# A decoder layer on one core: splits placed around the first softplus, first weights cast on VectorE in smaller first loads, and the products of the first step reordered

## The chip, the cores and the metric

The kernel runs on one core of one Trainium2 chip. The metric is the device time of one execution in microseconds, the median of several runs. Lower is better.

## The reference

The reference computes one layer of a hybrid decoder for 512 tokens and a model width of 1024, in fp32. One combined projection of the residual stream `x` gives the queries, keys and values of three causal mixers (differential attention, stick-breaking attention, dilated window attention) and three gate vectors. The branches are projected, gated and summed, go through an output projection and a LayerNorm, and then a squared-ReLU MLP and a gated input embedding follow, with a second LayerNorm. The change touches the start: the first columns of the projection, and the first head of stick-breaking attention.

```
proj = x @ w_in                                   # first columns used here: sb_q, sb_k, sb_v
z = einsum('bhqd,bhkd->bhqk', q, k) * d ** -0.5   # 8 heads, d = 64
log_keep = where(before, log_sigmoid(-z), 0)      # minus a softplus
later = reverse_cumsum(log_keep) - log_keep
a = where(before, exp(log_sigmoid(z) + later), 0)
out = a @ v
```

## The kernel before

**Splits.** Every fp32 matrix that TensorE multiplies is split in two fp32r halves: a high part (a copy that rounds) and a low part (the matrix minus its high part). A product is then three matmuls: high by high, high by low, low by high. For weights, `split_next` makes the high part `wh` on ScalarE (ACT, line 227) and the low part `wl` on VectorE (DVE, line 228), for a chunk of 128x1024 at a time. The raw chunks come by DMA on SyncE's queue (SP) into a ring of four buffers (`RAW`), and the halves go to a ring of seven (`RING`). `pump(limit, most)` writes out up to `most` splits, and `fill` the loads that fit.

**Items.** The program is a list of items. An item is one group of matmuls into a PSUM bank (`mm`) and the evacuation of that bank (`ev`), which is written out at the start of the next item. Most items use the two banks `mm`, so an item can begin only when the evacuation of the item before the last has read its bank. A chunk of weights is named here after what it feeds:

- item 0: `first_item`, the first two column tiles (queries and keys of head pair 0, "Q0" and "K0"). It takes its eight chunks of `x` and five loads of weights in turn (lines 296 to 324), 24 pairs of matmuls;
- item 1: Q1, and item 2: K1 (queries and keys of head pair 1), one chunk each, 24 matmuls each (lines 87 to 89);
- items 3 to 6: the stick-breaking values `sb_v` for four blocks of tokens, from four chunks V1 to V4 that all four items share (lines 337 to 339);
- items 7 to 10: Q2, K2, Q3, K3, one chunk each.

**Attention between the items.** `step()` runs generators of attention work, once at the start of each item from item 2 on and once in the middle of an item's matmuls. Head 0 of stick-breaking (`sb_head`) starts in the middle of item 1: it multiplies queries by keys into three banks and then computes a softplus for bank 2, and later (a half item or more each) for banks 1 and 0. A softplus is three passes on ACT (absolute value at line 1015, exponential at 1016, logarithm at 1017) and then a chain on DVE: line 1018 (sum `e`), 1021 (`sph`, the high part), 1022 (`spl`, the low part), and sums for the banks before it (lines 1031 to 1041). TensorE then multiplies these by triangular matrices (lines 1048 and 1052).

**Order.** A planner orders the instructions of each engine when the kernel is built: of those it believes ready, the one written first in the program goes first. Tiles of the common pool of 42 slots are handed out in the order of the program, so an evacuation that is written behind a softplus is also queued behind it. `tc.issue_after(i)` adds that what follows is queued behind `i` where it is on the same engine. The list `tie` holds the last ACT and the last DVE instruction of head 0's first softplus (bank 2), and `issue_split` queues each split behind these two; `tie` is emptied in item 4. The splits of V2 to V4, Q2, K2 and Q3 are written after that softplus, so they stand behind it, and they are free to stand between the softplus of bank 2 and those of banks 1 and 0.

**Start.** Nine bf16 matmuls on zeros (line 845) run while the first loads come. The loads from the fifth on wait for the fifth of these. Item 0 takes `x` chunk k, and with chunks 0, 1, 3, 5 and 7 a load of weights (256 columns with 0 and 7, 512 columns, for two k, with the others).

Of the kernel before, what the change touches and what calls it, by code (L numbers as in the profile page):

```python
# [55 lines left out]
def trunk(tc, a, out):  # L56
    nc = tc.nc
    es = ExitStack()
    with es:
# [23 lines left out]
        def at_bank():  # L83
            return psum.tile([P, 512], F32, name=nm("at"), tag="at", bufs=6)
# [62 lines left out]
        def load(src, w, own=False):  # L147
            s = {"src": src, "w": w, "uses": 0, "own": own}
            loads.append(s)
            return s  # L150
# [9 lines left out]
        def chunk_of(s):  # L160
            c = {"from": s, "w": s["w"]}
            s["uses"] += 1
            chunks.append(c)
            return c
# [50 lines left out]
        def split_next():  # L215
            c = chunks[st["split"]]
            w = c["w"]
            if c.get("dst") is None:
                h = ring.tile([P, 1024], F32R, name=nm("wh"), tag="wh", bufs=RING)
                lo = ring.tile([P, 1024], F32R, name=nm("wl"), tag="wl", bufs=RING)  # L220
                parts = [(h[:, :w], lo[:, :w], 0, w)]
                c["h"], c["l"] = parts[0][:2]
            else:
                parts = c["dst"]
            for h, lo, a0, a1 in parts:
                raw = c["from"]["raw"][:, a0:a1]
                nc.scalar.copy(h, raw)  # L227
                i = nc.vector.tensor_sub(lo, raw, h.bitcast(F32))  # L228
                st["low"] = getattr(i, "ins", i)
            c["from"]["uses"] -= 1  # L230
            st["split"] += 1
# [12 lines left out]
        def item(cs, mm, ev, need=None, bank=None):  # L244
            items.append({"c": cs, "mm": mm, "ev": ev, "need": need, "bank": bank})
# [55 lines left out]
        def first_item():  # L301

            w = a["w0"].rearrange("p k m -> p (k m)")
            cs = {}
            for k in range(8):
                x_chunk(k)
                if k in (0, 1, 3, 5, 7):
                    n = 256 if k in (0, 7) else 512
                    c = chunk_of(load(w[:, 256 * k:256 * k + n], n, True))
                    for i in range(n // 256):  # L310
                        cs[k + i] = (c, 256 * i)

            def mm(ps):
                for k in range(8):
                    c, o = cs[k]
                    for i, (m, x) in enumerate((("h", xh), ("l", xh), ("h", xl))):
                        for t in range(2):
                            nc.tensor.matmul(ps[t], c[m][:, o + t * P:o + t * P + P], x[k], start=k == 0 and i == 0,
                                             stop=k == 7 and i == 2, skip_group_check=True)

            def ev(ps):
                for t in range(2):
                    t_evac(*order[t][1:])(ps[t])
            item([cs[k][0] for k in (0, 1, 3, 5, 7)], mm, ev, bank=lambda: (at_bank(), at_bank()))

        def v_items(nv, name, g):
            cs = [chunk(a["wv"][nv, c].rearrange("p k n -> p (k n)"), 1024) for c in range(4)]
# [664 lines left out]
        def sb_head(hd):  # L992
            pr, side = hd // 2, hd % 2
            rs = (A, B)[side]
            while ("sb_q", pr) not in T or ("sb_k", pr) not in T:
                yield
            blk = [(0, 0, 0, 512), (1, 1, 0, 384), (2, 2, 0, 256), (3, 2, 256, 256)]
            bank = [at_bank() for _ in range(3)]
            for kb, bi, c0, n in reversed(blk):
                ps = bank[bi][:, c0:c0 + n]  # L1000
                mm_pair(ps, T["sb_k", pr], T["sb_q", pr], side, slice(kb * P, kb * P + P), slice(S - n, S),
                        kb != 2, False)
                if kb == 3:
                    nc.tensor.matmul(ps, identb, mask_b.rearrange("p a b -> p (a b)"), start=False, stop=False,
                                     skip_group_check=True)
                else:
                    nc.tensor.matmul(ps[:, 0:P], identb, mask_b[:, 1, :], start=False, stop=False,
                                     skip_group_check=True)
            w = [512, 384, 512]
            sph, spl, later = {}, {}, {}  # L1010
            for bi in (2, 1, 0):
                n = w[bi]
                ps = bank[bi][:, :n]
                e = slot("e")[:, :n]
                nc.scalar.activation(e, ps, AF.Abs)
                nc.scalar.activation(e, e, AF.Exp, scale=-1.0)
                ln = nc.scalar.activation(e, e, AF.Ln, bias=1.0)
                nc.vector.scalar_tensor_tensor(e, ps, 0.0, e, op0=OP.max, op1=OP.add)
                h = slot("sph", F32R)[:, :n]
                lo = slot("spl", F32R)[:, :n]  # L1020
                nc.vector.tensor_copy(h, e)
                low = nc.vector.tensor_sub(lo, e, h.bitcast(F32))
                if hd == 0 and bi == 2:

                    tie[:] = [getattr(i, "ins", i) for i in (ln, low)]
                sph[bi], spl[bi] = h, lo

                if bi == 2:
                    later[2] = (256, (h[:, HC], lo[:, HC]))
                    sm = slot("sm")[:, HB]  # L1030
                    nc.vector.tensor_add(sm, e[:, HB], e[:, HC])
                    hl = slot("smp", F32R)
                    nc.vector.tensor_copy(hl[:, HB], sm)
                    nc.vector.tensor_sub(hl[:, HC], sm, hl[:, HB].bitcast(F32))
                    later[1] = (256, (hl[:, HB], hl[:, HC]))
                elif bi == 1:
                    nc.vector.tensor_add(e[:, 128:384], e[:, 128:384], sm)
                    h = slot("smh", F32R)[:, :n]
                    lo = slot("sml", F32R)[:, :n]
                    nc.vector.tensor_copy(h, e)  # L1040
                    nc.vector.tensor_sub(lo, e, h.bitcast(F32))
                    later[0] = (384, (h, lo))
                yield
            ah, al = {}, {}
            for kb, bi, c0, n in reversed(blk):
                ps = bank[bi][:, c0:c0 + n]
                for hl in (sph, spl):
                    nc.tensor.matmul(ps, tri_r, hl[bi][:, c0:c0 + n], start=False, stop=False, skip_group_check=True)
                if kb < 3:
                    n2, hl = later[kb]  # L1050
                    for t in hl:
                        nc.tensor.matmul(bank[bi][:, c0 + n - n2:c0 + n], ones_r, t, start=False, stop=False,
                                         skip_group_check=True)
                if kb == 3:
                    continue
                n = w[bi]
                e = slot("a")[:, :n]
                nc.scalar.activation(e, bank[bi][:, :n], AF.Exp)
                h = slot("ah", F32R)[:, :n]
                lo = slot("al", F32R)[:, :n]  # L1060
                nc.vector.tensor_copy(h, e)
                nc.vector.tensor_sub(lo, e, h.bitcast(F32))
                ah[bi], al[bi] = h, lo
                if kb != 1:
                    yield
            while ("sb_v", 0, 3) not in V:
                yield
            po = at_bank()
            for kb, bi, c0, n in blk:
                v = V["sb_v", 0, kb][hd // 4][:, hd % 4]  # L1070
                nc.tensor.matmul(po[:, S - n:S], v.rearrange("p two d -> p (two d)"), ah[bi][:, c0:c0 + n],
                                 start=kb == 0, stop=False, skip_group_check=True)
                nc.tensor.matmul(po[A, S - n:S], v[:, 0, :], al[bi][:, c0:c0 + n], start=False, stop=kb == 3,
                                 skip_group_check=True)
            done = 4 + pr in oT
            if not done:
                oT[4 + pr] = slot("oT")
            t = slot("ot")
            nc.scalar.copy(t[A], po[B, :])
            nc.vector.tensor_add(oT[4 + pr][rs, :], po[A, :], t[A])  # L1080
            if done:
                split_sb(pr)
            yield
# [242 lines left out]
        for n, it in enumerate(items):  # L1326
# [9 lines left out]
            if prev is not None:  # L1336
                prev[0]["ev"](prev[1])

            pump(freed, 1 if n < 10 and n != 2 else 2)
            if n == 4:  # L1340
                tie.clear()
                with tc.issue_after(st["load"]):
                    load_consts()
            if n == 10:
# [128 lines left out]
```

## Time and profile before

| what | value |
|---|---|
| median of 3 runs | 1089.22 us (1088.9 to 1090.16) |
| the profiled execution | 1088.82 us |
| its span in the profile | 1087.1 us |
| TensorE busy | 1074.0 us, 99% of the span |
| VectorE, ScalarE busy | 691.8 us, 477.6 us |
| DMA | 105.71 MB, mean 97 GB/s |
| granted TensorE clock, mean | 0.996 |

The profiled execution lasted 1.72 us longer than its span and lies 0.40 us under the median. PE is TensorE's matmuls, PEld its weight loads. A line of the timeline gives the start, the duration, the engine, the line of the kernel, the operation, the tiles written and read, the shapes, and in brackets how long the engine was idle before it and what ended that idle time.

### The profile page before, as it was taken

Reading aid. Unit: us, or ns where it says so; the run is one execution under the profiler, and the core shown is the slowest. Engines: PE = TensorE matmul, PEld = TensorE weight load, DVE = VectorE, ACT = ScalarE, POOL = GpSimd, SP = SyncE. Lnnn points to the kernel's source line nnn. Section 1 sums busy time; section 2 is a strip of 40 time slices with the busy share of each in tenths; the row PEclk is TensorE's granted clock in tenths of the full one; section 3 lists DMA queues with packets and bytes.
Section 4 is the critical chain, followed back from the end, with each engine's and each line's share of the span. In section 5 each row is a group of like instructions: output and inputs, shape, how many; then the busy total and the mean of one; then the engine's idle time right before and its main releaser. Section 6 shows DMA issues by size and latency. Waiting matters only on the chain.

```text
span 1087.1 us, 13105 instructions
## 1 busy us (share of the span) xinstructions
PE 1074.0 (99%) x4991; PEld 894.2 (82%) x4991; DVE 691.8 (64%) x1245; ACT 477.6 (44%) x795; POOL 31.3 (3%) x55
## 2 busy tenths in 40 slices
PE   9899999999999999999999999999999999999997
PEld 6788788999888888888888888888888888888886
DVE  5788577657453757655444463866686686686676
ACT  6665445335232545454333232323554454454441
POOL 0000200000000000000000020110000000000000
PEclk9999999999999999999999999999999999999998
DMA  7432412031322113222233352253222422322402
GB/s 251 128 108 75 117 59 94 24 116 63 112 78 78 60 38 107 68 78 87 90 99 103 98 203 97 82 180 103 82 97 80 134 97 79 135 96 79 135 1 78
DMA packets 32431, 105.71 MB, mean 97 GB/s; under 512 B 4378, under 2 KB 5290, under 8 KB 32368
## 3 DMA queue, kind: packets, MB, share of 16 engines
q1 hardware_dynamic: 29424, 96.91, 27.4%
q0 software_dynamic: 2368, 7.05, 2.0%
q8 instruction: 39, 0.64, 0.2%
q10 hardware_dynamic: 576, 0.92, 0.2%
q14 instruction: 24, 0.20, 0.1%
HBM read 102.74 MB, written 2.12 MB: 96 GB/s over the span
## 4 chain that ended last, share of the span: by engine, by line
PE 94%; DVE 3%; DMA 1%; ACT 1%; issue 1%; DVEq 0%; SPq 0%
PE mm L87 17%; PE mm L89 17%; PE mm L88 17%; PE mm L337 3%; PE mm L339 3%; PE mm L338 3%; PE mm L679 2%; PE mm L681 2%; PE mm L680 2%; PE at L679 2%; PE at L681 2%; PE at L680 2%; PE mm L510 1%; PE mm L574 1%; PE mm L575 1%; PE mm L509 1%
## 5 line engine op out<-in xcount | busy, mean ns | idle before, releaser
L227 ACT CAST wh<-raw 128x1024 fp32r<-128x1024 f32 (+1 forms) x173 | 178.2, 1032 | 290.1 <-PE mm L88 222.8
L228 DVE TENSOR_TENSOR wl<-raw,wh 128x1024 fp32r<-128x1024 f32 (+1 forms) x173 | 206.1, 1196 | 104.6 <-ACT wh L227 100.6
L87 PE MATMUL mm<-xhT,wh 128*128 128x512 f32 x496 | 196.5, 396 | 0.0
L89 PE MATMUL mm<-xhT,wl 128*128 128x512 f32 x496 | 194.2, 391 | 0.1
L88 PE MATMUL mm<-xlT,wh 128*128 128x512 f32 x496 | 193.8, 391 | 0.0
L89 PEld LDWEIGHTS mm<-xhT,wl 128*128 128x128 f32 x496 | 93.1, 188 | 20.2 <-DVE wl L228 0.5
L87 PEld LDWEIGHTS mm<-xhT,wh 128*128 128x128 f32 x496 | 93.3, 188 | 19.5 <-issue 1.1
L88 PEld LDWEIGHTS mm<-xlT,wh 128*128 128x128 f32 x496 | 93.3, 188 | 17.8
L88 PE MATMUL mm<-x1lT,wh 128*128 128x512 f32 x256 | 99.6, 389 | 0.0
L89 PE MATMUL mm<-x1hT,wl 128*128 128x512 f32 x256 | 99.6, 389 | 0.0
L87 PE MATMUL mm<-x1hT,wh 128*128 128x512 f32 x256 | 99.6, 389 | 0.0
L337 PE MATMUL mm<-wh,xhT 128*128 128x512 f32 x160 | 65.5, 409 | 2.4 <-DVE sb_kb L108 2.3
L339 PE MATMUL mm<-wh,xlT 128*128 128x512 f32 x160 | 63.6, 398 | 0.0
L338 PE MATMUL mm<-wl,xhT 128*128 128x512 f32 x160 | 63.6, 397 | 0.0
L89 PEld LDWEIGHTS mm<-x1hT,wl 128*128 128x128 f32 x256 | 48.1, 188 | 10.1
L88 PEld LDWEIGHTS mm<-x1lT,wh 128*128 128x128 f32 x256 | 48.1, 188 | 10.0
L87 PEld LDWEIGHTS mm<-x1hT,wh 128*128 128x128 f32 x256 | 48.0, 188 | 9.9
L227 ACT CAST wh<-wsum 128x1024 fp32r<-128x1024 f32 x28 | 29.5, 1055 | 52.5 <-PE mm L88 49.3
L228 DVE TENSOR_TENSOR wl<-wsum,wh 128x1024 fp32r<-128x1024 f32 x28 | 34.2, 1222 | 24.2 <-ACT wh L227 23.6
L337 PEld LDWEIGHTS mm<-wh,xhT 128*128 128x128 f32 x160 | 38.2, 239 | 6.4 <-issue 2.7
L339 PEld LDWEIGHTS mm<-wh,xlT 128*128 128x128 f32 x160 | 38.3, 239 | 4.0
L338 PEld LDWEIGHTS mm<-wl,xhT 128*128 128x128 f32 x160 | 38.5, 241 | 3.5
(348 smaller groups left out, 1969.1 us busy)
## 6 DMA issues: line engine op xcount, KB each, us to landing
raw<-in_wt_dram SPq DMA_DIRECT2D x62, 512.0 KB, 3.4
raw<-in_wu_dram SPq DMA_DIRECT2D x32, 512.0 KB, 3.4
raw<-in_wd_dram SPq DMA_DIRECT2D x32, 512.0 KB, 3.3
raw<-in_wv_dram SPq DMA_DIRECT2D x20, 512.0 KB, 3.4
raw<-in_wb_dram SPq DMA_DIRECT2D x8, 512.0 KB, 3.3
raw<-in_wo_dram SPq DMA_DIRECT2D x8, 512.0 KB, 4.0
raw<-in_wg_dram SPq DMA_DIRECT2D x8, 512.0 KB, 3.9
rawx<-in_xT_dram SPq DMA_DIRECT2D x8, 256.0 KB, 5.1
```

Of the source, the lines that this page charges most:

```text
L87: nc.tensor.matmul(ps, wh, xh, start=start, stop=False, skip_group_check=True)
L88: nc.tensor.matmul(ps, wh, xl, start=False, stop=False, skip_group_check=True)
L89: nc.tensor.matmul(ps, wl, xh, start=False, stop=stop, skip_group_check=True)
L227: nc.scalar.copy(h, raw)
L228: i = nc.vector.tensor_sub(lo, raw, h.bitcast(F32))
L337: nc.tensor.matmul(ps, x1, c["h"][:, s], start=k == 0, stop=False)
L338: nc.tensor.matmul(ps, x1, c["l"][:, s], start=False, stop=False)
L339: nc.tensor.matmul(ps, x2, c["h"][:, s], start=False, stop=k == 7)
L509: nc.tensor.matmul(ps, h[:, q], c["l"][:, s], start=False, stop=False)
L679: nc.tensor.matmul(ps, h[:, q], c["h"][:, s], start=go, stop=False, skip_group_check=True)
L680: nc.tensor.matmul(ps, h[:, q], c["l"][:, s], start=False, stop=False, skip_group_check=True)
L681: nc.tensor.matmul(ps, lo[:, q], c["h"][:, s], start=False, stop=end, skip_group_check=True)
```

## The change

Three edits at the start of the kernel. First, the splits around head 0's softplus: item 1 writes out three of them instead of one (V1, V2, V3, ahead of the softplus of bank 2), item 2 one instead of two (V4), items 3 and 4 none, and items 5 to 8 one each (Q2, K2, Q3, K3). The first absolute value is queued behind the last cast written before it. `tie` is renewed by each of the three softplus of head 0 and emptied in item 8 instead of item 4, so that the splits of Q2, K2, Q3 and K3 are queued behind the softplus of bank 0. Second, in item 0 the first cast of weights moves from ACT to DVE, and the five loads of weights are 256, 256, 512, 512, 512 columns (with `x` chunks 0, 1, 2, 4, 6) instead of 256, 512, 512, 512, 256. Third, in item 0 the product of high weights by low `x` comes ahead of that of low weights by high `x`.

```diff
@@ split_next
-                nc.scalar.copy(h, raw)
+                i = nc.vector.tensor_copy(h, raw) if c.get("dve") else nc.scalar.copy(h, raw)
+                st["cast"] = getattr(i, "ins", i)
@@ first_item
-                if k in (0, 1, 3, 5, 7):
-                    n = 256 if k in (0, 7) else 512
+                if k in (0, 1, 2, 4, 6):
+                    n = 256 if k < 2 else 512
                     c = chunk_of(load(w[:, 256 * k:256 * k + n], n, True))
+                    c["dve"] = k == 0
...
-                    for i, (m, x) in enumerate((("h", xh), ("l", xh), ("h", xl))):
+                    for i, (m, x) in enumerate((("h", xh), ("h", xl), ("l", xh))):
...
-            item([cs[k][0] for k in (0, 1, 3, 5, 7)], mm, ev, bank=lambda: (at_bank(), at_bank()))
+            item([cs[k][0] for k in (0, 1, 2, 4, 6)], mm, ev, bank=lambda: (at_bank(), at_bank()))
@@ sb_head
-                nc.scalar.activation(e, ps, AF.Abs)
+                with ExitStack() as behind:
+                    if hd == 0 and bi == 2:
+
+                        behind.enter_context(tc.issue_after(st["cast"]))
+                    nc.scalar.activation(e, ps, AF.Abs)
...
-                if hd == 0 and bi == 2:
+                if hd == 0:
 
                     tie[:] = [getattr(i, "ins", i) for i in (ln, low)]
@@ the loop over items
-            pump(freed, 1 if n < 10 and n != 2 else 2)
+            pump(freed, {1: 3, 3: 0, 4: 0}.get(n, 1 if n < 10 else 2))
+            if n == 8:
+                tie.clear()
             if n == 4:
-                tie.clear()
                 with tc.issue_after(st["load"]):
                     load_consts()
```

## The prediction

> **What bounds the kernel now.** I read the page first, then the list of who waited for whom on PE, then the timelines around the waits that it names, and the busy times by stretch.
>
> ```profile
> PE 1074.0 (99%) x4991; PEld 894.2 (82%) x4991; DVE 691.8 (64%) x1245; ACT 477.6 (44%) x795; POOL 31.3 (3%) x55
> ```
>
> PE is the bound: an edit that takes no matmul away gains only where PE stands still or runs slowly. The list of waits says where that is:
>
> ```profile
> PE mm L337 <- DVE sb_kb L108: 2.3, 1, 2.3
> PE at L845 <- DVE rel L881: 1.3, 1, 1.3
> PE at L1048 <- DVE spl L1022: 0.9, 1, 0.9
> PE at L318 <- ACT wh L227: 0.4, 1, 0.4
> ```
>
> The second line is the start before any work. The other three lie in the first 44 us, in the places that the diff touches. Busy time by stretch (columns: PE, PEld, DVE, ACT, POOL, granted clock, DMA share, GB/s) shows a further price behind them:
>
> ```profile
> 31.00:39.50 8.50, 8.37 (x45) 6.73 (x43) 8.34 (x13) 7.73 (x14) 0.00 (x0) 1.00 0.62 201
> 39.50:47.20 7.70, 4.51 (x14) 3.25 (x13) 6.92 (x14) 2.20 (x5) 0.00 (x0) 0.78 0.74 226
> 47.20:60.00 12.80, 12.80 (x58) 10.64 (x57) 6.83 (x15) 5.20 (x11) 0.00 (x0) 1.00 0.01 2
> ```
>
> From 39.5 to 47.2 PE is busy for 4.51 of 7.70 us and its mean clock is 0.78. At half clock for a share s the mean is 1 - s/2, so s = 0.44, or 3.4 us; in these half the work is lost, 1.7 us. So the place costs 0.92 + 2.27 + 1.7 = 4.9 us. From 47.2 on PE is full and at full clock.
>
> Why DVE was late is in its timeline:
>
> ```profile
> 27.46 0.69 DVE L1018 SCALAR_TENSOR_TENSOR e<-at,e 128x512 f32<-128x512 f32 x1 [2.26 <-ACT e L1017]
> ...
> 34.74 2.36 DVE L228 TENSOR_TENSOR wl<-raw,wh 128x1024 fp32r<-128x1024 f32 x2
> 37.13 0.56 DVE L1018 SCALAR_TENSOR_TENSOR e<-at,e 128x384 f32<-128x384 f32 x1
> 37.60 1.21 DVE L228 TENSOR_TENSOR wl<-raw,wh 128x1024 fp32r<-128x1024 f32 x1
> 38.73 0.35 DVE L1021 CAST sph<-e 128x384 fp32r<-128x384 f32 x1
> 39.00 1.22 DVE L228 TENSOR_TENSOR wl<-raw,wh 128x1024 fp32r<-128x1024 f32 x1
> 40.14 0.55 DVE L1022 TENSOR_TENSOR spl<-e,sph 128x384 fp32r<-128x384 f32 x1
> ...
> 42.85 0.69 DVE L108 SCALAR_TENSOR_TENSOR sb_kb<-mm,sb_kb 64x512 fp32r<-64x512 f32 x1
> ```
>
> DVE is idle for 2.26 us ahead of the first softplus and then busy without a break up to the evacuation of K1 (`sb_kb`), which frees the bank for item 4. Among these are six subtractions of splits. In the order of the program they are V2 (29.59), V3 (30.93), V4 and Q2 (the two at 34.74), K2 (37.60) and Q3 (39.00). Q2, K2 and Q3 are not needed before item 7.
>
> **The change, part by part.** *Splits of Q2, K2, Q3 out of the way.* From start to next start they hold DVE for 1.2 (half of 37.13 - 34.74), 1.13 and 1.14 us: 3.47 us. Behind the softplus of bank 0 they stand behind K1's evacuation too. `sb_kb` then ends at 43.54 - 3.47 = 40.07. PE ends item 3 at 39.5; it has 0.6 us of bank 1's products (two of 384 columns at 0.18, two of 256 at 0.12) and so asks for the bank at 40.1 if they stay there, at 39.5 if not. The wait is 0 to 0.6 us instead of 2.27, from this alone. `spl` of bank 1 ends at 40.69 - 3.47 = 37.2, ahead of the 39.7 at which PE asks for it: the 0.92 goes.
>
> *V2 and V3 ahead of the softplus.* ACT was idle from 23.1 to 25.50, where it began the absolute value (idle 2.38 us). Two casts at 3.89/4 = 0.97 us fit in, if the raw data is there: V3's load was issued at 18.56, and at 3.4 us to landing (the page's median) it is there at 22.0. So the wait that is added for the absolute value costs nothing; without that cover the softplus slips by up to 1.95 us, and behind it on ACT wait its other two passes, V4's cast and the evacuations of Q1 and K1. On DVE the two subtractions (1.13 each) fall into its idle 2.26 us, give or take 0.2. All that follows, K1's evacuation too, moves up by up to 2.26 us, to 37.8. Both bounds together: `sb_kb` ends between 37.8 and 40.1, and PE needs it between 39.5 and 40.1. I take no wait, since the idle stretch of DVE is a row of this trace and V2's data was long there.
>
> *No wait, no half clock.* With both waits under 0.6 us the clock has no reason to drop: a wait of 0.92 us (39.83 to 40.74) was followed by matmuls of normal length, and only the second one by slow ones. The 1.7 us go too. The page "TensorE: Matmul & The Clock Gate" of the Trainium skill (What's actually happening) has the clock halved after an idle window of about 3.4 us, and its section on why this matters warns only of idle gaps above about 3 us; here 2.27 us, with 0.92 us just before it, was enough, and the measurement decides.
>
> *Where the moved splits go.* Q2, K2 and Q3 now follow bank 0's `spl` on DVE, which ends 1.8 us behind `sb_kb` (1018, 1021, 1022: 0.69 + 0.43 + 0.69), at 39.6 to 41.9. In that part of the old trace DVE was idle for 3.55 + 0.44 + 1.41 + 0.38 = 5.8 us (47.9 to 59.8), which covers 3.47. Their loads are earlier than before or not needed until item 7, and SP's queue, with the constants that item 4 puts there, waits for no later split than V4's. What is late next is the evacuation of item 3 (`sb_v`), 0.85 us on DVE: it is done by 41.9 + 0.85 = 42.8, or, if all three splits go first, 46.2. PE asks for that bank at 39.5 + 0.6 + 24 matmuls at 0.227 = 45.5. So 0 to 0.7 us; I take 0.2, nearer to 0 since the evacuation is written first.
>
> *The start.* Item 0 begins when `x` and the first weights are both cast.
>
> ```profile
> 5.35 1.11 PE L318 MATMUL at<-xhT,wh 128*128 128x512 f32 x2
> ...
> 16.22 1.05 ACT L227 CAST wh<-raw 128x1024 fp32r<-128x1024 f32 x1 [0.70 <-DMA raw<-in_wt_dram]
> ...
> 17.30 1.22 DVE L228 TENSOR_TENSOR wl<-raw,wh 128x1024 fp32r<-128x1024 f32 x1 [1.02 <-ACT wh L227]
> ...
> 18.58 0.19 PEld L89 LDWEIGHTS mm<-xhT,wl 128*128 128x128 f32 x1 [0.54 <-DVE wl L228]
> ```
>
> On DVE a cast of this size takes 0.28 us (line 1033) and runs beside ACT's cast of `x`: the first matmul comes at about 5.05, 0.3 us earlier. With k = 1 the cast is 0.40 instead of 0.62: 0.22 us earlier. The new order of products saves waits for `wl` (about 0.1 to 0.3 in k = 0 and 1) and puts no operand later than it was. Up to 0.5 us, then; but item 1 ends this: its third matmul waited for the low half of its own weights, whose raw data landed at 16.2, and these follow the same 3 MB as before. Item 0 ending earlier only makes that wait longer. Below nothing: 128 KB less is on the way before the held-back loads start, and at the 321 GB/s of 4 to 5 us that is 0.4 us later for all that follows. Bounds -0.3 and +0.4 us; I take 0.
>
> Sum: -4.9 + 0.2 + 0 = -4.7 us against the profiled execution's 1088.82, which makes 1084.1; with the 0.40 us by which the median lies higher, 1084.5.
>
> **The rivals.**
> - *The moved splits come back at the values' evacuation.* The planner may put all three splits ahead of `sb_v`. Against it: the program has the evacuation first. For it: the evacuation goes ACT, DVE, ACT, DVE, and leaves gaps that a split of 1.2 us fills. Price 0.7 us without a drop of the clock, up to 2.27 + 1.7 = 4.0 with one: 1085.0 to 1088.3, middle 1086.7.
> - *K1's evacuation lands behind bank 0's softplus.* Then `sb_kb` is 1.8 us later, 39.6 to 41.9; a wait of 0.1 to 2.4 us remains, the longer one with the clock's 1.7. Of the 4.9 us between 4.8 and 0.8 are gained: up to 1088.4. Against it: its place in the program is ahead, and the old trace kept it.
> - *Slower: a wait at every value item.* PE comes 5 us earlier to the same DVE work, and DVE is busy for 17.3 of 20 us from 60 to 80. If DVE's backlog frees a bank later than 45.5 + 2.3 = 47.8 us, the clock drops, at 4.0 us each; it decides from the second such wait: -4.9 + 8.0 = +3.1, 1092.3. For it: the low idle time of DVE there. Against it: the 5.8 us of idle before 60, and PE never waited after 47 at the same load. By the skill's 3 us the clock would stay and each wait cost 2.3.
> - *No change at all*, because the order of the planner does not follow the ties: 1089.2. The old trace shows the splits just where the tie puts them, so this is unlikely.
>
> **How the numbers follow.** Forecast 0.68 (1083.0 to 1086.0: the start's bounds, a wait of up to 1.3 us, and 0.9 us on the lower side for the 1.3 us over which the three runs spread). First rival 0.12, second 0.06, slower 0.11, no change 0.03. The range from 1083.0 to 1087.5 takes the forecast and most of the first two rivals, about 0.8. About 0.2% (2.2 us) is what a measurement of this kernel can tell from no change. Under 1087.0 lie the forecast and over half of the first two rivals: faster 0.78; same 0.11; slower 0.11.
>
> **What would show it.** Right: no wait of PE on `sb_kb` or on `spl` between 30 and 50 us; a clock of 1.00 there; no subtraction of a split on DVE between `e` of bank 1 and `sb_kb`; two casts on ACT ahead of the first absolute value, which starts near 25.5; item 1's third matmul still waiting for its `wl` near 18.5. Wrong: a clock under 1.00 after 20 us, a PE wait on `sb_v`, or the first absolute value after 27 us.

## The result, and the profile after

The changed kernel takes 1083.7 us (median of 5 runs, 1082.99 to 1083.78) against 1089.22 us before (1087.84 to 1090.16 over 5 runs). The ratio is 0.9947, with a 95% interval from 0.9933 to 0.9962: 5.5 us less. The profiled execution took 1083.78 us with a span of 1082.1 us, 5.0 us shorter than the span before. In every batch below the kernel before ran beside the others on the same chip; its medians there were 1088.4 to 1088.9 us.

The page has PE a little less busy and the other engines as before, so no work went away:

```profile
PE 1070.5 (99%) x4991; PEld 892.7 (83%) x4991; DVE 691.8 (64%) x1246; ACT 477.5 (44%) x794; POOL 31.3 (3%) x55
```

The list of waits on PE (engine and line that waited, what it waited for, then the total, the number and the longest in us):

```profile
PE at L320 <- ACT wh L227: 1.8, 1, 1.8
PE at L847 <- DVE rel L883: 1.3, 1, 1.3
PE at L138 <- DVE sb_ka L108: 0.5, 1, 0.5
PE at L1124 <- DVE lg L1119: 0.2, 1, 0.2
```

The waits on `spl` and on `sb_kb` are gone. In their place stand a longer one at the start (1.8) and a new one of 0.5 us on `sb_ka`, the evacuation of K0. The stretches of the prediction (PE, PEld, DVE, ACT, POOL, granted clock, DMA share, GB/s):

```profile
31.00:39.50 8.50, 8.50 (x46) 6.90 (x45) 8.11 (x16) 6.75 (x11) 0.00 (x0) 1.00 0.39 119
39.50:47.20 7.70, 7.70 (x36) 6.45 (x35) 6.98 (x12) 3.03 (x7) 0.00 (x0) 1.00 0.44 142
47.20:60.00 12.80, 12.80 (x58) 10.34 (x58) 10.05 (x17) 8.62 (x14) 0.00 (x0) 1.00 0.34 105
```

From 39.5 to 47.2 PE is busy for all of 7.70 us instead of 4.51, and the clock is 1.00 instead of 0.78. DVE's timeline from the softplus of bank 1 on shows why:

```profile
34.65 0.56 DVE L1024 SCALAR_TENSOR_TENSOR e<-at,e 128x384 f32<-128x384 f32 x1
35.24 0.36 DVE L1027 CAST sph<-e 128x384 fp32r<-128x384 f32 x1
35.64 0.56 DVE L1028 TENSOR_TENSOR spl<-e,sph 128x384 fp32r<-128x384 f32 x1
...
38.36 0.69 DVE L108 SCALAR_TENSOR_TENSOR sb_kb<-mm,sb_kb 64x512 fp32r<-64x512 f32 x1
...
40.88 1.22 DVE L229 TENSOR_TENSOR wl<-raw,wh 128x1024 fp32r<-128x1024 f32 x1
42.02 0.42 DVE L352 TENSOR_TENSOR sb_v<-mm,sb_v 128x256 fp32r<-128x256 f32 x1
42.35 1.22 DVE L229 TENSOR_TENSOR wl<-raw,wh 128x1024 fp32r<-128x1024 f32 x1
43.48 0.42 DVE L352 TENSOR_TENSOR sb_v<-mm,sb_v 128x256 fp32r<-128x256 f32 x1
43.82 1.22 DVE L229 TENSOR_TENSOR wl<-raw,wh 128x1024 fp32r<-128x1024 f32 x1
```

No subtraction of a split stands between `e` of bank 1 and `sb_kb`. `sb_kb` ends at 39.05; item 4's first matmul starts at 40.23 without a wait, so 1.18 us are to spare. Q2, K2 and Q3 (the three at line 229) come after it and are interleaved with the two halves of `sb_v`'s evacuation, which ends at 43.90. PE comes to that bank 24 matmuls of 0.227 us after 40.23, at 45.7.

### The profile page after: what moved, and what is told of

It is laid out like the page before. It is cut to its first block, busy times and chain, and to the rows that moved or that the text cites. A ratio compares the mean times of both kernels' runs of the same rounds, so it can differ in the third digit from the quotient of the medians.

```text
span 1082.1 us, 13108 instructions
## 1 busy us (share of the span) xinstructions
PE 1070.5 (99%) x4991; PEld 892.7 (83%) x4991; DVE 691.8 (64%) x1246; ACT 477.5 (44%) x794; POOL 31.3 (3%) x55
## 3 DMA queue, kind: packets, MB, share of 16 engines
HBM read 102.74 MB, written 2.12 MB: 97 GB/s over the span
## 4 chain that ended last, share of the span: by engine, by line
PE 96%; DVE 2%; ACT 1%; DMA 0%; issue 0%; DVEq 0%; SPq 0%
PE mm L87 17%; PE mm L88 17%; PE mm L89 17%; PE mm L339 3%; PE mm L341 3%; PE mm L340 3%; PE mm L681 2%; PE mm L683 2%; PE mm L682 2%; PE at L681 2%; PE at L683 2%; PE at L682 2%; PE mm L512 1%; PE mm L576 1%; PE mm L577 1%; PE mm L511 1%
```

## The experiments

**Each part alone.** *splits_only* is the changed kernel with item 0 as it was before (first cast on ACT, loads of 256, 512, 512, 512, 256 columns, old order of products). *start_only* is the kernel before with the new item 0 alone.

> The changed kernel with item 0 as it was before (loads of 256, 512, 512, 512, 256 columns, first cast on ACT, old order of products): only the splits, the ties and the queued absolute value are new. Theory 1 (the gain is PE's two waits, 0.92 and 2.27 us, and the 1.7 us at half clock): 1084.0 to 1084.7, no wait of PE on sb_kb or spl, clock 1.00 after the start. Rival (the start edits carry 1 us or more of the 5.5 us): 1085.0 or more, with the same clean stretch from 30 to 50 us.

> The kernel before with the new item 0 alone (smaller first loads, first cast on DVE, new order of products). Theory 1: 1088.8 to 1089.6, no change, because item 1 waits for its own weights or the loads end item 0; the waits near 40 and 42 us and a clock of one half stay. Rival (the start carries a part of the gain): 1088.2 or less, PE ahead by 0.5 us or more when item 1 ends.

Measured: splits_only 1083.05 us (1082.47 to 1083.41), ratio 0.995 [0.9935, 0.9965]. start_only 1089.42 us (1086.98 to 1090.8), ratio 1.0008 [0.9999, 1.0018]. The whole gain is in the splits. The new start brings nothing. By medians the kernel that has it even lies higher, by 0.6 us with the new splits and by 0.5 us without them, both inside the intervals. The waits on PE in start_only:

```profile
PE mm L339 <- DVE sb_kb L108: 2.3, 1, 2.3
...
PE at L1050 <- DVE spl L1024: 0.9, 1, 0.9
PE at L138 <- DVE sb_ka L108: 0.5, 1, 0.5
PE mm L339 <- DVE sb_qlb L108: 0.4, 1, 0.4
```

The two old waits are there unchanged, and the 0.5 us on `sb_ka` comes with the new start, since splits_only has no such wait. The last line is a wait of item 3 on Q1's evacuation; the kernel before has it too, without its list showing it (below).

**Each half of the splits alone.** *tie_only* renews `tie` after each of head 0's softplus and empties it in item 8, with the splits written where they were. *pump_only* does the opposite: new numbers of splits, `tie` as before, and the first absolute value not queued behind a cast. Both have the old start.

```diff
# tie_only, against before
-                if hd == 0 and bi == 2:
+                if hd == 0:
                     tie[:] = [...]
...
+            if n == 8:
+                tie.clear()
             if n == 4:
-                tie.clear()
# pump_only, against before
-            pump(freed, 1 if n < 10 and n != 2 else 2)
+            pump(freed, {1: 3, 3: 0, 4: 0}.get(n, 1 if n < 10 else 2))
```

> The kernel before with the new ties alone: the number of splits written per item is as before, so V2 and V3 stay behind the first softplus, V4 and Q2 go behind that of bank 1 and K2 and Q3 behind that of bank 0. Two subtractions of 1.13 us leave the time ahead of K1's evacuation: sb_kb ends at 43.5 - 2.3 = 41.2 and PE asks at 40.1, a wait of about 1.1 us; no wait on spl. Theory 1 with a clock that stays at such a wait: 1089.2 - 0.9 - 1.2 - 1.7 = 1085.4. If a wait of 1.1 us lowers the clock: 1087.1.

> The kernel before with the new numbers of splits per item alone, without the new ties and without queuing the absolute value: V2 and V3 come ahead of the first softplus, Q2, K2 and Q3 are written later but the planner still puts them between the softplus of bank 2 and K1's evacuation. 2.26 us leave the chain on DVE: sb_kb ends at 41.3, a wait of about 1.2 us. Theory 1: 1085.3 with the clock up, 1087.0 with it down. Rival (writing them later is enough and the ties do nothing): 1084.2, no wait at all.

Measured: tie_only 1084.41 us (1084.33 to 1084.8), ratio 0.9962 [0.995, 0.9975]; pump_only 1084.88 us (1084.01 to 1084.98), ratio 0.9964 [0.9951, 0.9977]. One line of each list of waits, tie_only first:

```profile
PE mm L338 <- DVE sb_kb L108: 1.0, 1, 1.0
```

```profile
PE mm L338 <- DVE sb_kb L108: 1.3, 1, 1.3
```

Neither waits on `spl` any more, and in neither does the clock drop. So each half is worth most of the gain by itself (4.5 and 4.0 of the 5.8 us of splits_only): each brings `sb_kb` early enough to remove one wait, shorten the other and keep the clock. Only the last 1.4 to 1.8 us (by medians) need both: the rest of the wait on `sb_kb`, and 0.3 us at item 3 that both kernels still lose (below).

*q2k2q3_only* asks whether it is enough to write Q2, K2 and Q3 later, with V2, V3 and the ties as before.

```diff
# against before
-            pump(freed, 1 if n < 10 and n != 2 else 2)
+            pump(freed, {2: 2, 3: 0, 4: 0}.get(n, 1 if n < 10 else 2))
```

> The kernel before with only the numbers of splits of items 3 to 8 from the change (Q2, K2, Q3, K3 written out later), V2 and V3 where they were, the ties as before. Theory 1: without ties the planner pulls the three subtractions back to between the softplus of banks 1 and 0, so nothing moves: 1089.2 us, with waits on spl (0.9) and sb_kb (2.3) and the low clock. Rival (writing them later is enough): 1084.4 us as with the ties alone.

Measured: 1088.53 us (1087.98 to 1089.4), ratio 1.0001 [0.9991, 1.001], with the waits of before:

```profile
PE mm L338 <- DVE sb_kb L108: 2.3, 1, 2.3
...
PE at L1049 <- DVE spl L1023: 0.9, 1, 0.9
```

Without a tie the planner pulls the three subtractions back to where they stood. This fits the planner's rule, by which the place in the program decides only among what it believes ready. So pump_only's gain is that of V2 and V3 ahead of the softplus, and the gain of the late splits comes from the ties.

**The price of one wait.** *wait4* and *wait5* are the changed kernel with four and five extra subtractions on DVE ahead of K1's evacuation; their results are used by nothing.

```diff
# wait4, against the changed kernel, at the evacuation of K1
+                    with tc.issue_after(tie[1]):
+                        for _ in range(4):
+                            i = nc.vector.tensor_sub(junk, xh[0].bitcast(F32), xl[0].bitcast(F32))
+                    with tc.issue_after(getattr(i, "ins", i)):
+                        T[name, j] = evac_stacked(ps, name, sc)
```

> The changed kernel with four more subtractions of 128x512 on DVE (0.69 us each, results unused) queued between bank 1's softplus and K1's evacuation: sb_kb ends 2.8 us later, at 41.85, and TensorE, which asks at 40.23, waits 1.6 us. Theory 1 (a wait costs its length, and the clock drops only behind a longer wait or two in a row): clock 1.00, time 1083.7 + 1.6 = 1085.3 us. Rival (any wait over about 1.5 us halves the clock for 3.4 us): 1087.0 us with a granted clock near 0.8 from 40 to 48 us. Second rival (the wait is caught up later, behind TensorE's own backlog): 1083.7 us.

> The changed kernel with five more such subtractions, and the planner then puts the sum e of bank 0 ahead of K1's evacuation too: sb_kb ends 4.2 us later, at 43.2, and TensorE waits 3.0 us. Theory 1: the clock drops behind a single wait of this length as it did before the change: 1083.7 + 3.0 + 1.7 = 1088.4 us, granted clock near 0.8 in the 8 us from the wait on. Rival (the clock dropped before only because two waits came within 4 us): clock 1.00, 1086.7 us.

Measured: wait4 1085.23 us (1084.37 to 1085.64), with a wait of 1.48 us and the clock at 1.00. wait5 1088.23 us (1085.43 to 1089.99 in 10 runs), ratio 0.9998 [0.9989, 1.0007], with a wait of 2.67 us. Both medians are those of theory 1. The extra subtractions give back the whole gain, so the lateness of K1's evacuation is enough as a cause. How the clock behaves is best seen in stretches cut where the trace changes the granted clock. The kernel before, then wait4, then wait5, in the columns of the stretches above:

```profile
40.34:43.76 3.42, 0.74 (x4) 0.57 (x4) 3.26 (x7) 0.52 (x2) 0.00 (x0) 1.00 0.92 257
43.76:47.17 3.41, 3.41 (x8) 2.66 (x9) 2.81 (x6) 0.87 (x2) 0.00 (x0) 0.50 0.51 170
```

```profile
37.34:40.76 3.42, 2.04 (x11) 1.59 (x9) 3.29 (x6) 0.81 (x2) 0.00 (x0) 1.00 0.00 0
40.76:44.17 3.41, 3.31 (x15) 2.76 (x16) 3.34 (x6) 0.04 (x1) 0.00 (x0) 1.00 0.00 0
```

```profile
41.99:45.41 3.42, 0.75 (x5) 0.53 (x4) 3.33 (x7) 0.20 (x1) 0.00 (x0) 1.00 0.00 0
45.41:48.82 3.41, 3.41 (x10) 2.63 (x9) 3.38 (x6) 0.87 (x2) 0.00 (x0) 0.50 0.07 10
```

In each kernel the stretches between changes of the clock are whole multiples of 3.413 us (before: 11 of them at full clock, then one at half; start_only 11 and two). In the windows of this grid PE was idle, before the drop, for 2.67 us in the kernel before and in wait5, and for 1.38 us in wait4, where the clock stayed.

**The start.** *after_k1_first* puts K1's cast back ahead of item 0's evacuations in ACT's queue. *after_old_loads* is the changed kernel with the old sizes of the first loads. *best_mix* has both, and *after_again* is the changed kernel once more, all in one batch; *best_again* is the mix once more in a later one.

```diff
# after_k1_first, against the changed kernel, in first_item
             def ev(ps):
-                for t in range(2):
-                    t_evac(*order[t][1:])(ps[t])
+                with tc.issue_after(st["cast"]):
+                    for t in range(2):
+                        t_evac(*order[t][1:])(ps[t])
# after_old_loads, against the changed kernel
-                if k in (0, 1, 2, 4, 6):
-                    n = 256 if k < 2 else 512
+                if k in (0, 1, 3, 5, 7):
+                    n = 256 if k in (0, 7) else 512
```

> The changed kernel, with item 0's evacuations queued behind K1's cast on ACT (as ScalarE had them before the change). Theory 1: the new item 0 let the planner start Q0's first evacuation ahead of K1's cast, which makes K0's evacuation 0.75 us later and TensorE wait 0.5 us for sb_ka at 25.3 us; with the cast first that wait is gone, the first absolute value starts near 25.7 instead of 26.26, and the time is 1083.2 us. Rival: K1's cast is needed just as urgently by the second item, or another operand is late next in the same place (sb_qlb, or the raw keys): the time stays at 1083.7 us.

> The changed kernel with the first five loads of weights as before (256, 512, 512, 512, 256 columns), but with the first cast on DVE and the new order of products. Theory 1: the sizes of the first loads move the first 10 us only, item 1's end is set by the raw data behind them, so the time is that of the changed kernel, 1083.7 us within 0.5. The wait of 0.5 us for sb_ka stays, since ACT's queue still has Q0's first evacuation ahead of K1's cast. Rival: the smaller first loads pay, and without them the time is 0.4 us or more above the changed kernel, 1084.1 us or more.

> The changed kernel with both: the loads as before and K1's cast ahead of item 0's evacuations; the first cast on DVE and the new order of products stay. Theory 1: like the changed kernel's splits with the old start, which took 1083.05 us: 1083.0 us, no wait of TensorE on sb_ka. Rival (the first cast on DVE is worth the 0.3 us by which the first matmul comes earlier): 1082.7 us.

> The changed kernel once more, beside the three variants of its start on one chip. Theory 1: 1083.7 us, 0.5 us above the two variants with K1's cast first. Rival (the start's differences are those from execution to execution): no order among the four, all within 0.5 us.

> The mix of the splits as changed, the old sizes of the first loads, the first cast on DVE, the new order of products and K1's cast ahead of item 0's evacuations, once more. Theory 1: 0.5 us are gained over the changed kernel by the missing wait on sb_ka and the rest of its 1082.57 us was a lucky start: 1083.2 us. Rival: the whole 1.2 us is a property of this order: 1082.6 us again.

| kernel | median, range (5 runs each) | ratio to before | wait on `sb_ka` | item 1's third matmul |
|---|---|---|---|---|
| after_again | 1083.79 (1083.38 to 1083.86) | 0.9955 [0.9943, 0.9968] | 0.5 | 18.69 |
| after_old_loads | 1083.65 (1083.08 to 1083.96) | 0.9954 [0.9942, 0.9967] | 0.5 | 18.83 |
| after_k1_first | 1083.51 (1083.47 to 1084.78) | 0.9956 [0.9943, 0.997] | none | 18.82 |
| best_mix | 1082.57 (1082.48 to 1084.57) | 0.9949 [0.9936, 0.9961] | none | 18.27 |
| best_again (same kernel, later batch) | 1082.67 (1082.37 to 1082.76) | 0.9944 [0.993, 0.9957] | none | 18.42 |

The sizes of the first loads change nothing that can be measured, as expected. With K1's cast first the wait on `sb_ka` is gone, but by medians only 0.3 of the 0.5 us show: in its profile item 1's third matmul waited 0.3 us for its low weights instead. The mix lies 1.1 us under the changed kernel in two batches, 9 of its 10 runs under all 5 of after_again, and its profile repeats the earlier third matmul; for it, theory 1 of the repeat fell and the rival held. The intervals of the ratios overlap, so that it beats the changed kernel is likely rather than settled. It is the fastest version that was run. Some 0.7 us of its lead is the missing wait on `sb_ka` (0.66 us from start to start of the matmuls around it) and 0.3 to 0.4 the earlier third matmul.

Why the old sizes help only together with K1's cast first has no run of its own, but the profiles suggest a reason. Q1's cast starts when its raw chunk lands: at 15.08 and 15.16 in the two profiles of the mix, at 16.46 in after_k1_first, where item 1 then waited for the low half made from it. Over all profiles it starts at 14.93 to 15.26 with the old sizes (in that of the kernel before at 16.22) and at 15.65 to 17.00 with the new ones. In after_old_loads it started at 15.26 as well, but there item 0 ended only at 18.38, so item 1 had no use for it.

## Why the prediction was right, and where its steps were off

**The place and its price.** Predicted were 4.9 us at the waits on `spl` and `sb_kb`, less 0.2 later. From the start of the 101st matmul to that of the 201st (the same kinds and numbers of matmuls in both) the kernel before took 53.78 - 27.34 = 26.44 us, the changed one 48.75 - 27.88 = 20.87: 5.57 us. From there to the end of the span both take 1033.3 us, so the gain lies here. The term was sized too low by some 0.7 us. A matmul of 512 columns has 0.39 us in its row, but the next one starts 0.227 us after it. So behind a wait some 0.16 us of overlap are lost that the list of waits does not count: 0.3 us for two waits. From start to start, the two gaps lost 1.07 and 2.43 us instead of 0.92 and 2.27. Most of the rest is a third wait, which the sum left out; the list of waits of the kernel before does not name it. Item 3 needs the bank that Q1's evacuation frees. Before:

```profile
33.10 0.69 DVE L108 SCALAR_TENSOR_TENSOR sb_qlb<-mm,sb_qb 64x512 fp32r<-64x512 f32 x1
...
33.58 0.23 PE L1007 MATMUL at<-mask_b,identb 128*128 128x128 bf16 x1
...
33.95 0.47 PE L337 MATMUL mm<-wh,xhT 128*128 128x512 f32 x1
```

The last two starts lie 0.36 us apart. In the changed kernel the same two lie 0.04 apart (34.14 and 34.18), with that evacuation done at 33.71. tie_only and pump_only still have the gap (0.36 and 0.37 us): in each, two subtractions of splits stand between the first softplus and Q1's evacuation, as before, in the changed kernel one. So 1.07 + 2.43 + 1.7 + 0.32 = 5.5 of the 5.57 us are accounted for. Another 0.2 of the forecast is the wait on `sb_v` that was charged and did not come.

**Splits out of the way, V2 and V3 into idle time.** `sb_kb` ended at 39.05, inside the predicted 37.8 to 40.1, and tie_only and pump_only show that both edits did their share. The cover also held: the two subtractions and the two casts went into idle time. ACT then had 0.40 us left:

```profile
26.26 0.60 ACT L1021 ACTIVATE e<-at 128x512 f32<-128x512 f32 x1 [0.40 <-PE at L1009]
```

But the first absolute value started at 26.26, not near 25.5, and what ended ACT's idle time is PE, which gave the products later.

**The start.** This is the step that failed in its working. The bounds were -0.3 and +0.4 us, and 0 was taken; at its 101st matmul the changed kernel was 0.54 us later. The first matmul came at 4.89 (5.05 predicted, 5.35 before), and k = 1 began at 6.50 instead of 7.77. All of that was lost in one wait up to 9.94 for k = 2, whose raw data landed late. Its length varies between profiles of the same kernel: 1.8 us here and 1.3 in after_again, 0.6 and 1.9 in the two profiles of the mix. The old start has such a wait too, 0.4 us in the profile of before and 1.1 in that of splits_only, so the forecast was measured from a profile with a short one. Item 1's third matmul started at 18.73 against 18.59, and it did not wait for its low weights as predicted, because item 0 itself ended later (18.27 against 17.85). The larger part, about 0.5 us, came behind that, and what the sum left out there is ACT's queue:

```profile
18.25 0.59 ACT L125 ACTIVATE sb_qa<-at 64x512 fp32r<-64x512 f32 x1 [0.92 <-PE at L320]
18.74 1.03 ACT L227 CAST wh<-raw 128x1024 fp32r<-128x1024 f32 x1
```

Before, K1's cast ran at 17.50 and the evacuations of item 0 behind it. In the changed kernel the planner put Q0's first evacuation ahead of K1's cast. The cast then stands between Q0's two evacuations, K0's on DVE come 0.76 us later (24.55 instead of 23.79), and PE waits for `sb_ka`. after_old_loads keeps the old sizes and still has the wait, so it is the cast on DVE or the order of products that turned the queue; the two were not tried apart. The cost, 0.5 to 0.6 us, took most of what the place gave beyond its predicted size, so the sum came out closer than its terms. That is luck.

**No half clock.** Right in its result: the clock stays at 1.00 from 5.1 us to past the last matmul. That short waits leave the clock alone holds here, but the length of a wait, alone or with the one before it, is not what decides; the last section tells what the runs show instead.

**The rivals.** The splits did come between the halves of `sb_v`'s evacuation, as the first rival has it, but the bank was free at 43.90 and asked for at 45.7: 1.8 us of slack, no price. K1's evacuation stayed ahead of bank 0's softplus. No value item waits: PE is busy for the whole of 50 to 100 us, and from the 201st matmul on both kernels take the same time. That the planner follows the ties is shown by tie_only, and by q2k2q3_only from the other side.

## What to carry to other kernels

Before an edit is costed, list what stands in the queue ahead of the evacuation that frees the next bank; here moving work behind it, or into idle time ahead of it, brought 4.5 and 4.0 us by itself, and both together 5.8. Where a planner orders the queues, write the order as a dependency, since a later place in the program alone moved nothing here. And an edit that takes work off an engine can change the order in that engine's queue: ask what its next two instructions will be.

## What the runs showed of the hardware

The granted clock changes on a grid of 3.413 us whose phase differs from execution to execution, and it is decided by how much of one window PE stands idle, not by the length of a wait (idle times are gaps between the rows of matmuls, whose ends are modelled, and "end" is the time behind the last one):

| profile | window from (us) | PE idle in it | share | clock of the next window |
|---|---|---|---|---|
| before | 40.34 | 2.67 us | 78% | half |
| wait5 | 41.99 | 2.67 us | 78% | half |
| q2k2q3_only | 40.11 | 2.62 us | 77% | half |
| wait5, start | 7.86 | 2.12 us | 62% | half |
| before, end | 1077.99 | 2.03 us | 60% | half |
| start_only | 39.56 | 1.92 us | 56% | half |
| best_mix, end | 1071.43 | 1.72 us | 50% | full |
| best_again, start | 4.70 | 1.67 us | 49% | full |
| after_old_loads, start | 6.12 | 1.58 us | 46% | full |
| after, start | 8.51 | 1.43 us | 42% | full |
| wait4 | 37.34 | 1.38 us | 40% | full |
| pump_only | 38.38 | 1.31 us | 38% | full |

So the limit lies between 50 and 56% of a window in these profiles; every other window at full clock held 37% or less and was followed by full clock, or, behind the last matmul, 67% or more and was followed by half. The length of a wait does not give this order: in start_only the clock dropped at 42.97, when the second wait had lasted 1.00 us and the first one had been 0.91, while single waits of 1.48 us (wait4) and 1.87 (best_again) were followed by no drop. Of the 0.92 us on `spl` in the kernel before only 0.4 fell into the window that decided; the 2.27 us on `sb_kb` alone would have been 67%. A window that is already at half clock stayed there in start_only behind 1.26 us of idle time (37%). A wait can then cost nothing beyond its length, or 1.7 us more, or, as in start_only, some 2.8 (half of the 2.15 us in which PE worked in the first low window, and 1.7 in the second), depending on where the grid falls. In wait5 the run with a mean clock of 0.999 took 1085.43 us, the seven with 0.996 or 0.997 took 1087.65 to 1088.67, and the two with 0.994 took 1089.98 and 1089.99; the profile above is of one of these two and has two low windows. This is also a large part of the spread of the kernel before: beside the experiments, its runs with a mean clock of 0.999 took 1086.59 to 1087.12 us, those with 0.995 1089.16 to 1090.36.

The Trainium skill, "TensorE: Matmul & The Clock Gate" (What's actually happening), has a free-running window of 3413 ns, which the grid of every profile here bears out. It drops the clock after an idle window; here a window that was idle for 56% was enough.
